# Attention's values: one TensorE product for both parts of the probabilities, with the parts' rows turned on ScalarE and added on GpSimd

## The chip, the cores and the metric

The kernel runs on one core of a Trainium2 chip. The metric is the time of one execution in device microseconds (us), the median of three. The core's engines work side by side: TensorE (PE) multiplies, VectorE (DVE), ScalarE (ACT) and GpSimd (POOL) do the elementwise work, SyncE (SP) issues the transfers.

## The reference

One decoder layer for one sequence of 256 positions, width 1024, all in float32. Cut to what matters here:

```
proj  = x @ w_in                       -> q | k | v | B | C | h | gate_attn | gate_conv
y_att = attention(q, k, v) @ W_att     8 heads of 64, causal, one block of 256 keys
y_cnv = (B * causal_dwconv3(C * h)) @ W_cnv
mix   = (sigmoid(g_att) * y_att + sigmoid(g_cnv) * y_cnv) @ W_o
x     = LayerNorm(alpha * x + mix)
u     = causal_dwconv3(x @ W_up);  f = (silu(u_gate) * u_val) @ W_down
x     = LayerNorm(alpha * x + f)
```

With 256 positions there is no earlier block, so attention is softmax(q k^T / 8) v over the keys up to the query's own position. The step that is changed is the last product of it: probabilities times values, and how its result gets from PSUM to the operand `aT` of the product with W_att.

## The kernel before

**Two parts of every operand.** To keep float32 accuracy with TensorE's shorter format, each operand is split into a high part (a copy, which rounds) and a low part (what the rounding left). For weights ScalarE makes the high part `wh` (line 221 of the profile) and VectorE the low part `wl` (line 231), from the loaded `raw`. `mm3` then makes three products: high by high, high by low, low by high (lines 336, 337, 338). The operands on the other side (`xT`, `yT`, `aT`, `mT`, `x1T`) are split in the same way: high on ScalarE, low on VectorE (lines 250 and 254).

**Units and slots.** The weights are a list of units of 128 rows by 1024 words. `slot(u)` writes one unit's TensorE products and then, in a fixed order, what the other engines do beside them: ScalarE's work of the slot's first half ("act"), the next `wh`, ScalarE's second half ("act2"), VectorE's first half ("first"), the next `wl`, VectorE's second half ("dve"). Each engine runs its own list strictly in this order; a wait holds all that stands behind it. The table `STEPS` says in which half-slot (twice the unit's number, plus one for a second half) each stage of attention, of the convolution and of the gates stands. Units 0 to 11 of this table are the products for h, C and B, units 12 to 27 those for the gates `g`, from 28 on those for `y` (y_att and y_cnv), then come W_o (`o`), and the feed-forward part (`u`, `d`, `e`).

**Attention's values.** The eight heads go in four pairs p of two heads j. `vp[:, t, p, js]` holds, for 128 keys (t), 128 columns: 64 of V's high part and 64 of its low part. `PT[:, a, j, :]` holds the transposed probabilities of head j, high part (a = 0) and low part (a = 1): 256 queries for the first 128 keys, 128 queries for the second. `attend(p)` makes eight products per pair into one PSUM bank: for each head, both parts of the probabilities with 256 words, and both with 128, all summed onto each other. The result has 128 rows: the upper 64 from V's high part, the lower 64 from V's low part. `attend_out` (ScalarE) copies the lower 64 rows of both heads to the upper rows of a scratch tile `ac`; `attend_sum` (VectorE) adds them to the upper rows that are still in PSUM, one head to each half of the tile's rows; `attend_h` (ScalarE) and `attend_l` (VectorE) make `aT`'s two parts from it. The attention products stand in the slots of units 13, 19, 22 and 24.

**What is near in the program.** `m` (line 874) sums the gated branches on VectorE; ScalarE puts `m` into 16-bit halves (`mix`, line 880), a transposing transfer turns them, ScalarE joins them (`mw`, line 888) and makes `mT`; TensorE's W_o products read `mT`. Behind those come the first LayerNorm and `x1T`, which the feed-forward products read. GpSimd does little: memsets, three masks (`affine_select`), one power per LayerNorm (`pow`, line 968), and four adds of `fs` near the end (line 1315).

Of the kernel before, what the change touches and what calls it, by code (L numbers as in the profile page):

```python
# [13 lines left out]
AF = mybir.ActivationFunctionType  # L14
ALU = mybir.AluOpType

P = 128
S = 256
# [3 lines left out]
HD = 64  # L22
# [128 lines left out]
def layer_kernel(ctx: ExitStack, tc: tile.TileContext, x, wpack, cpack, b_gate, ln1_g, ln1_b, ln2_g, ln2_b, out):  # L151
    nc = tc.nc
# [13 lines left out]
    def ps_bank(name):  # L166
        return ps_pool.tile([P, 512], F32, tag="ps", name=name)

    def scratch(shape, name, bufs=None, tag="scr"):
        return tmp.tile(shape, F32, tag=tag, name=name, bufs=bufs or 5)  # L170
# [190 lines left out]
    vp = vpt[:, 0:2048].rearrange("p (t g n) -> p t g n", t=2, g=4)  # L361
    PT = vpt[:, 2048:3584].rearrange("p (a j n) -> p a j n", a=2, j=2)
# [51 lines left out]
    SB, SM, PR = {}, {}, {}  # L414
# [77 lines left out]
    def attend(p):  # L492


        o = PR[p, "o"] = ps_bank(f"av{p}").rearrange("p (j s) -> p j s", j=2)
        for j in range(2):
            js = slice(j * P, (j + 1) * P)
            for a in range(2):
                nc.tensor.matmul(o[:, j], vp[:, 0, p, js], PT[:, a, j, 0:256], start=a == 0, stop=False)
            for a in range(2):  # L500
                nc.tensor.matmul(o[:, j, P:S], vp[:, 1, p, js], PT[:, a, j, 256:384], start=False, stop=a == 1)

    def attend_out(p):

        c = PR[p, "c"] = scratch([P, 2, S], f"ac{p}")
        nc.scalar.activation(c[0:HD], PR[p, "o"][HD:P], AF.Copy)

    def attend_sum(p):
        c, o = PR[p, "c"], PR[p, "o"]
        nc.vector.tensor_tensor(c[HD:P, 0], o[0:HD, 1], c[0:HD, 1], op=ALU.add)  # L510
        nc.vector.tensor_tensor(c[0:HD, 0], o[0:HD, 0], c[0:HD, 0], op=ALU.add)

    def attend_h(p):
        nonlocal aT
# [11 lines left out]
    def at(u, part, f, *a):  # L526
        beside.setdefault(u, {}).setdefault(part, []).append((f, a))
# [44 lines left out]
    def open_ps():  # L572
# [5 lines left out]
    STEPS = dict(vl=[3, 0],  # L578
             qw=[5, 7, 9, 13],
             qwE=[1, 1, 1, 0],  # L580
             qh=[7, 9, 11, 14],
             ql=[6, 9, 12, 16],
             s=[5, 11],
             m=[13, 17, 23, 24],
             e=[15, 21, 24, 31],
             n=[17, 23, 33, 37],
# [4 lines left out]
             av=[13, 19, 22, 24],  # L591
             out=[26, 39, 44, 49],
             sum=[35, 42, 49, 51],
             ah=[41, 47, 50, 54],
             al=[44, 52, 53, 55],
             c1=[21, 35],
             c2a=[23, 26, 38, 41],
             c2d=[25, 29, 41, 44],
# [16 lines left out]
    def on(engine, step, f, *a):  # L615
        u, part = divmod(step, 2)
        at(C0 + u, (("act", "act2"), ("first", "dve"))[engine][part], f, *a)
# [13 lines left out]
    for p in range(4):  # L631
        on(1, STEPS["m"][p], masked, p)
        on(0, STEPS["e"][p], exps, p)
        on(1, STEPS["n"][p], normalize, p)
        on(1, STEPS["n"][p], probs_halves, p)
        on(1, STEPS["n"][p], probs_T, p)
        on(STEPS["wE"][p], STEPS["w"][p], probs_words, p)
        on(0, STEPS["h"][p], probs_h, p)
        on(1, STEPS["l"][p], probs_l, p)
        at(C0 + STEPS["av"][p], "pe", attend, p)  # L640
        on(0, STEPS["out"][p], attend_out, p)
        on(1, STEPS["sum"][p], attend_sum, p)
        on(0, STEPS["ah"][p], attend_h, p)
        on(1, STEPS["al"][p], attend_l, p)

# [600 lines left out]
    for k, (kind, i, u) in enumerate(seq[:tail_from]):  # L1246
        if k == half_steps:
            hold.clear()
        if kind == "h":
            c, v, t = i  # L1250
# [11 lines left out]
        elif kind == "u":  # L1262
            c, v = i
# [142 lines left out]
```

## Time and profile before

| what | value |
|---|---|
| median of three runs | 354.62 us (354.11 to 354.84) |
| profiled execution | 354.48 us |
| its span, first to last instruction | 352.7 us |
| PE busy | 345.2 us (98%), 1603 products |
| DVE busy | 298.9 us (85%) |
| ACT busy | 245.7 us (70%) |
| POOL busy | 8.4 us (2%) |
| mean granted TensorE clock | 0.997 |

The profile comes from one execution, 354.48 us long; 1.8 us of it lie outside the span. "Busy" is the time in which an engine had an instruction in work. A row of a timeline gives the start, the time from the first start to the last end of the instructions put together in it, the engine, the line, the operation, the tile it writes and those it reads, the shape, the count, and in brackets how long the engine was idle before it and who released it. Matmuls are pipelined, so a product's row is longer (0.39 us) than the distance to the next one.

### The profile page before, as it was taken

How to read it: one execution, taken by the hardware profiler on the slowest of the kernel's cores; microseconds unless marked ns; L12 is line 12 of the kernel's file. 1: busy time of each engine (PE TensorE's matmuls, PEld its weight loads, DVE VectorE, ACT ScalarE, POOL GpSimd, SP SyncE). 2: the span in 40 equal slices, each digit the busy share in tenths (PEclk: the TensorE clock that was granted, in tenths of full speed). 3: DMA queues.
4: the chain of work that ended last, by engine and by line, in shares of the span. 5: the costliest groups of instructions: out<-in, count | busy, mean ns of one | idle time of the engine just before them, and what ended most of it. 6: DMA issues, size and time to landing. Idle time of an engine off the chain costs nothing.

```text
span 352.7 us, 4599 instructions
## 1 busy us (share of the span) xinstructions
PE 345.2 (98%) x1603; PEld 287.0 (81%) x1603; DVE 298.9 (85%) x508; ACT 245.7 (70%) x370; POOL 8.4 (2%) x29
## 2 busy tenths in 40 slices
PE   9999999999999999999999999999999999999992
PEld 8788888888888888888888888888888888888882
DVE  4797787999989998879867879999999879796985
ACT  3776948789896767856496658688686867758700
POOL 1000000000001000000100000000000000000120
PEclk9999999999999999999999999999999999999998
DMA  7999886779867899993298199779969987753002
GB/s 250 422 418 362 181 282 243 147 271 226 199 185 242 336 367 256 315 259 119 47 305 186 24 335 309 284 162 315 321 128 413 260 256 242 200 210 61 0 30 90
DMA packets 56070, 81.63 MB, mean 231 GB/s; under 512 B 45552, under 2 KB 46192, under 8 KB 49008
## 3 DMA queue, kind: packets, MB, share of 16 engines
q1 hardware_dynamic: 56048, 81.35, 74.1%
q8 instruction: 12, 0.20, 0.2%
q14 instruction: 10, 0.08, 0.1%
HBM read 69.28 MB, written 1.05 MB: 199 GB/s over the span
## 4 chain that ended last, share of the span: by engine, by line
PE 90%; issue 3%; DVE 3%; ACT 2%; POOL 1%; POOLq 0%; DVEq 0%
PE u L336 11%; PE u L337 11%; PE u L338 11%; PE qk L677 6%; PE g L336 4%; PE g L337 4%; PE g L338 4%; PE v L677 3%; PE d L337 3%; PE d L336 3%; PE d L338 3%; PE o L338 2%; PE o L337 2%; PE y L338 2%; PE y L337 2%
## 5 line engine op out<-in xcount | busy, mean ns | idle before, releaser
L231 DVE TENSOR_TENSOR wl<-raw,wh 128x1024 fp32r<-128x1024 f32 x104 | 125.0, 1217 | 15.6 <-ACT wh L221 15.4
L221 ACT ACTIVATE wh<-raw 128x1024 fp32r<-128x1024 f32 x102 | 103.9, 1051 | 3.4 <-DMA raw<-in_wpack 3.4
L336 PE MATMUL u<-wh,x1T 128*128 128x512 f32 x176 | 68.5, 389 | 0.0
L337 PE MATMUL u<-wl,x1T 128*128 128x512 f32 x176 | 68.5, 389 | 0.0
L338 PE MATMUL u<-wh,x1T 128*128 128x512 f32 x176 | 68.5, 389 | 0.0
L338 PEld LDWEIGHTS u<-wh,x1T 128*128 128x128 f32 x176 | 33.0, 188 | 6.9
L336 PEld LDWEIGHTS u<-wh,x1T 128*128 128x128 f32 x176 | 33.0, 188 | 6.9
L337 PEld LDWEIGHTS u<-wl,x1T 128*128 128x128 f32 x176 | 33.0, 188 | 6.8
L1050 ACT ACTIVATE fc<-pb,consts 128x256 f32<-128x256 f32 x44 | 20.0, 503 | 24.0 <-DVE pb L1092 24.0
L336 PE MATMUL d<-wh,f 128*128 128x512 f32 x76 | 29.6, 389 | 0.0
L337 PE MATMUL d<-wl,f 128*128 128x512 f32 x76 | 29.6, 389 | 0.0
L338 PE MATMUL d<-wh,f 128*128 128x512 f32 x76 | 29.6, 389 | 0.0
L1083 ACT ACTIVATE up<-u 128x1024 uint16<-128x1024 uint16 x22 | 21.4, 1012 | 6.2 <-PE u L338 6.2
L336 PE MATMUL g<-wh,xT 128*128 128x512 f32 x64 | 25.3, 395 | 0.0
L337 PE MATMUL g<-wl,xT 128*128 128x512 f32 x64 | 25.0, 390 | 0.0
L338 PE MATMUL g<-wh,xT 128*128 128x512 f32 x64 | 24.9, 389 | 0.0
L1058 DVE SCALAR_TENSOR_TENSOR fc<-pb,consts,fc 128x254 f32<-128x254 f32 x44 | 21.3, 483 | 1.6
L1056 DVE SCALAR_TENSOR_TENSOR fc<-pb,consts,fc 128x255 f32<-128x255 f32 x44 | 21.0, 477 | 0.9 <-ACT fc L1050 0.9
L254 DVE TENSOR_TENSOR wl<-raw,wh 128x512 fp32r<-128x512 f32 (+2 forms) x23 | 20.4, 929 | 1.6 <-ACT wh L253 1.4
L253 ACT ACTIVATE wh<-raw 128x512 fp32r<-128x512 f32 (+2 forms) x23 | 17.6, 815 | 2.5 <-DMA raw<-in_wpack 2.5
L677 PE MATMUL qk<-wh,xT 128*128 128x512 f32 x60 | 19.2, 390 | 0.0
L1092 DVE COPY pb<-up 128x1024 uint16<-128x1024 uint16 x22 | 16.5, 749 | 1.9 <-DMA up<-up 1.8
(207 smaller groups left out, 608.7 us busy)
## 6 DMA issues: line engine op xcount, KB each, us to landing
raw<-in_wpack SPq DMA_DIRECT2D x55, 1024.0 KB, 5.6
raw<-in_wpack SPq DMA_DIRECT2D x6, 896.0 KB, 11.4
bg<-in_b_gate SPq DMA_DIRECT2D x4, 256.0 KB, 5.1
xr<-in_x SPq DMA_DIRECT2D x1, 1024.0 KB, 8.3
ln<-in_ln_g SPq DMA_DIRECT2D x2, 512.0 KB, 6.3
ln<-in_ln_b SPq DMA_DIRECT2D x2, 512.0 KB, 7.1
raw<-in_wpack SPq DMA_DIRECT2D x3, 256.0 KB, 4.0
raw<-in_wpack SPq DMA_DIRECT2D x1, 512.0 KB, 6.3
```

The source lines that it names most:

```text
L221: nc.scalar.activation(units[u]["h"], raw_of(u), AF.Copy)
L231: nc.vector.tensor_tensor(units[u]["l"], raw_of(u), units[u]["h"].bitcast(F32), op=ALU.subtract)
L253: nc.scalar.activation(h, src, AF.Copy)
L254: (eng or nc.vector).tensor_tensor(l, src, h.bitcast(F32), op=ALU.subtract)
L336: nc.tensor.matmul(o, ah, bh, start=start, stop=False)
L337: nc.tensor.matmul(o, ah, bl, start=False, stop=False)
L338: nc.tensor.matmul(o, al, bh, start=False, stop=stop)
L677: nc.tensor.matmul(banks[m][t], (xl if p == 2 else xh)[:, k, t * P:(t + 1) * P], wl if p == 1 else wh, start=k == 0 and p == 0, stop=k == ...
L1050: nc.scalar.activation(PB["c", i][:, a], PB[i][:, a * S:(a + 1) * S], AF.Copy, scale=w_ffn(2, j))
L1056: nc.vector.scalar_tensor_tensor(c[:, 1:S], pb[:, a * S:a * S + S - 1], w_ffn(1, j), c[:, 1:S], op0=ALU.mult, op1=ALU.add)
L1058: nc.vector.scalar_tensor_tensor(c[:, 2:S], pb[:, a * S:a * S + S - 2], w_ffn(0, j), c[:, 2:S], op0=ALU.mult, op1=ALU.add)
L1083: nc.scalar.activation(half.rearrange("p (w n) -> p w n", w=2), PB["rows", c][t].bitcast(U16).rearrange("p (n w) -> p w n", w=2), AF.Copy)
```

## The change

`attend` now gives each head a bank of its own and streams both parts of the probabilities through the columns of V in one product: 512 words for the first 128 keys, and two runs of 128 words for the second. The bank then holds, side by side, the sums with the probabilities' high part and with their low part, 128 rows each. `attend_out` copies the low-part halves of both heads to `ac` (two ScalarE copies of 128 rows by 256), `attend_sum` adds the high-part halves to them (two VectorE adds of 128 rows by 256). A new function `attend_turn` brings the lower 64 rows of `ac` up (one ScalarE copy, 64 rows by 512) and adds them to the upper ones in two GpSimd adds of 64 rows by 256; head 1's result goes to the lower half of the rows as before. `STEPS` places `attend_turn`, and places `attend_h` and `attend_l` anew. Other lines move down by 8 (L231 stays, L841 becomes L849, and so on).

```
     def attend(p):
-        o = PR[p, "o"] = ps_bank(f"av{p}").rearrange("p (j s) -> p j s", j=2)
+        o = PR[p, "o"] = [ps_bank(f"av{p}_{j}").rearrange("p (a s) -> p a s", a=2) for j in range(2)]
         for j in range(2):
             js = slice(j * P, (j + 1) * P)
-            for a in range(2):
-                nc.tensor.matmul(o[:, j], vp[:, 0, p, js], PT[:, a, j, 0:256], start=a == 0, stop=False)
-            for a in range(2):
-                nc.tensor.matmul(o[:, j, P:S], vp[:, 1, p, js], PT[:, a, j, 256:384], start=False, stop=a == 1)
+            nc.tensor.matmul(o[j], vp[:, 0, p, js], PT[:, :, j, 0:256], start=True, stop=False)
+            nc.tensor.matmul(o[j][:, :, P:S], vp[:, 1, p, js], PT[:, :, j, 256:384], start=False, stop=True)
     def attend_out(p):
         c = PR[p, "c"] = scratch([P, 2, S], f"ac{p}")
-        nc.scalar.activation(c[0:HD], PR[p, "o"][HD:P], AF.Copy)
+        for j in range(2):
+            nc.scalar.activation(c[:, j], PR[p, "o"][j][:, 1], AF.Copy)
     def attend_sum(p):
         c, o = PR[p, "c"], PR[p, "o"]
-        nc.vector.tensor_tensor(c[HD:P, 0], o[0:HD, 1], c[0:HD, 1], op=ALU.add)
-        nc.vector.tensor_tensor(c[0:HD, 0], o[0:HD, 0], c[0:HD, 0], op=ALU.add)
+        for j in range(2):
+            nc.vector.tensor_tensor(c[:, j], o[j][:, 0], c[:, j], op=ALU.add)
+    def attend_turn(p):
+        c = PR[p, "c"]
+        low_rows = scratch([P, 2, S], f"al{p}")
+        nc.scalar.activation(low_rows[0:HD], c[HD:P], AF.Copy)
+        for j in (1, 0):
+            nc.gpsimd.tensor_tensor(c[j * HD:j * HD + HD, 0], c[0:HD, j], low_rows[0:HD, j], op=ALU.add)
...
-             ah=[41, 47, 50, 54],
-             al=[44, 52, 53, 55],
+             turn=[36, 44, 50, 52],
+             ah=[41, 48, 53, 56],
+             al=[44, 52, 56, 57],
...
+        on(0, STEPS["turn"][p], attend_turn, p)
```

On TensorE, the values of the first pair stand between two products of the gates; these were the rows before (`av` is the bank, `vpt` holds V's columns and the probabilities):

```order
L499 MATMUL av_875<-vpt 128x256 x2
L501 MATMUL av_875<-vpt 128x128 x2
L499 MATMUL av_875<-vpt 128x256 x2
L501 MATMUL av_875<-vpt 128x128 x2
```

And these stand in the same place now:

```order
L498 MATMUL av_0_875<-vpt 128x512
L499 MATMUL av_0_875<-vpt 128x2x128
L498 MATMUL av_1_876<-vpt 128x512
L499 MATMUL av_1_876<-vpt 128x2x128
```

Eight products became four, with as many words in all; nothing else on TensorE moved.

On VectorE, this is the stretch from the sums of the third pair on, before (`ac_1050`, `ac_1124` and `ac_1187` are the scratch tiles of the second, third and fourth pair; 128x1024 rows are weights' low parts):

```order
L510 TENSOR_TENSOR ac_1187<-av_1170,ac_1187 64x256
L511 TENSOR_TENSOR ac_1187<-av_1170,ac_1187 64x256
L250 TENSOR_TENSOR aT<-ac_1050,aT 128x256
L231 TENSOR_TENSOR wl_1233<-raw_1046,wh_1185 128x1024
L250 TENSOR_TENSOR aT<-ac_1124,aT 128x256
L250 TENSOR_TENSOR yT<-ct_1044,yT 128x2x256
L231 TENSOR_TENSOR wl_1254<-raw_1046,wh_1230 128x1024
L250 TENSOR_TENSOR aT<-ac_1187,aT 128x256
L841 TENSOR_TENSOR gates<-g_1156,bg_1101 128x512
L841 TENSOR_TENSOR gates<-g_1157,bg_1101 128x512
L231 TENSOR_TENSOR wl_1270<-raw_1093,wh_1251 128x1024
```

And now (`ac_1049`, `ac_1125`, `ac_1186` are the same three pairs):

```order
L510 TENSOR_TENSOR ac_1186<-av_0_1171,ac_1186 128x256
L510 TENSOR_TENSOR ac_1186<-av_1_1172,ac_1186 128x256
L250 TENSOR_TENSOR aT<-ac_1049,aT 128x256
L231 TENSOR_TENSOR wl_1241<-raw_1045,wh_1184 128x1024
L250 TENSOR_TENSOR yT<-ct_1043,yT 128x2x256
L231 TENSOR_TENSOR wl_1260<-raw_1045,wh_1237 128x1024
L250 TENSOR_TENSOR aT<-ac_1125,aT 128x256
L849 TENSOR_TENSOR gates<-g_1157,bg_1101 128x512
L849 TENSOR_TENSOR gates<-g_1158,bg_1101 128x512
L231 TENSOR_TENSOR wl_1277<-raw_1093,wh_1257 128x1024
L250 TENSOR_TENSOR aT<-ac_1186,aT 128x256
```

VectorE has as many instructions as before. The low part of `aT` for the third pair moved behind `yT` and a weight; that for the fourth pair behind two gate adds and a weight.

On ScalarE, this is the stretch of the third and fourth pair now (`al` is the tile of the turned rows; L523 writes `aT`'s high part, L852 the gates):

```order
L505 ACTIVATE ac_1186<-av_0_1171 128x256
L505 ACTIVATE ac_1186<-av_1_1172 128x256
L515 ACTIVATE al_1210<-ac_1125 64x512
L814 ACTIVATE yT<-ct_1043 128x2x256
L852 ACTIVATE gates<-gates 128x512 x2
L515 ACTIVATE al_1233<-ac_1186 64x512
L221 ACTIVATE wh_1237<-raw_1045 128x1024
L523 ACTIVATE aT<-ac_1125 128x256
L221 ACTIVATE wh_1257<-raw_1093 128x1024
L523 ACTIVATE aT<-ac_1186 128x256
```

The turning copies (L515) are new, the copies out of PSUM (L505) are two per pair in place of one, and each high part of `aT` stands one weight or more behind the turn that feeds it.

## Rows read from the trace of the kernel before

**Rows 1.** The page: busy time of the engines, share of the span, instructions.

```profile
PE 345.2 (98%) x1603; PEld 287.0 (81%) x1603; DVE 298.9 (85%) x508; ACT 245.7 (70%) x370; POOL 8.4 (2%) x29
```

**Rows 2.** Windows: stretch, length, busy time of PE, PEld, DVE, ACT, POOL.

```profile
106.10:122.70 16.60, 16.60 (x83) 14.02 (x82) 16.51 (x24) 11.86 (x18) 1.16 (x2) 1.00 0.78 281
```

**Rows 3.** Timeline of TensorE around the first pair's values.

```profile
79.37 0.39 PE L338 MATMUL g<-wh,xT 128*128 128x512 f32 x1
...
80.29 0.34 PE L501 MATMUL av<-vpt 128*128 128x128 f32 x2
80.46 0.45 PE L336 MATMUL g<-wh,xT 128*128 128x512 f32 x1
80.75 0.40 PE L337 MATMUL g<-wl,xT 128*128 128x512 f32 x1
80.98 0.39 PE L338 MATMUL g<-wh,xT 128*128 128x512 f32 x1
```

**Rows 4.** Timeline of TensorE at products of 256 words, near the end.

```profile
344.13 0.28 PE L1178 MATMUL e<-wl,f 128*128 128x256 f32 x1
...
344.49 0.28 PE L1178 MATMUL e<-wl,f 128*128 128x256 f32 x1
```

**Rows 5.** Timeline of VectorE, from before the second pair's sums to behind the fourth pair.

```profile
97.91 0.69 DVE L250 TENSOR_TENSOR yT<-ct,yT 128x512 fp32r<-128x512 f32 x1 [1.26 <-ACT yT L806]
...
103.09 0.99 DVE L795 SCALAR_TENSOR_TENSOR ct<-z,consts,ct 128x256 f32<-128x256 f32 x2
104.10 0.42 DVE L510 TENSOR_TENSOR ac<-av,ac 64x256 f32<-64x256 f32 x1
104.53 0.42 DVE L511 TENSOR_TENSOR ac<-av,ac 64x256 f32<-64x256 f32 x1
...
111.67 2.44 DVE L231 TENSOR_TENSOR wl<-raw,wh 128x1024 fp32r<-128x1024 f32 x2
...
121.07 0.41 DVE L250 TENSOR_TENSOR aT<-ac,aT 128x256 fp32r<-128x256 f32 x1
121.40 1.27 DVE L841 TENSOR_TENSOR gates<-g,bg 128x512 f32<-128x512 f32 x2
122.60 1.20 DVE L231 TENSOR_TENSOR wl<-raw,wh 128x1024 fp32r<-128x1024 f32 x1
```

**Rows 6.** Timeline of ScalarE: the second pair's copy out of PSUM.

```profile
107.10 0.59 ACT L506 ACTIVATE ac<-av 64x512 f32<-64x512 f32 x1 [1.33 <-PE av L501]
```

**Rows 7.** GpSimd by line and shape: count | busy us, mean ns | idle before.

```profile
L1315 POOL TENSOR_TENSOR fs<-fs 128x256 f32<-128x256 f32 x3 | 2.2, 738 | 163.9 <-ACT fs L1312 163.8
L1315 POOL TENSOR_TENSOR fs<-fs 128x128 f32<-128x128 f32 x1 | 0.5, 462 | 0.1
```

**Rows 8.** Timeline of GpSimd: a mask alone, one beside VectorE's work, and the adds.

```profile
1.29 0.29 POOL L270 TENSOR_SCALAR_AFFINE_SELECT mask<-mask 128x128 f32<-128x128 f32 x1
...
112.08 0.95 POOL L953 TENSOR_SCALAR_AFFINE_SELECT ident<-ident 128x128 f32<-128x128 f32 x1
...
334.12 2.79 POOL L1315 TENSOR_TENSOR fs<-fs 128x256 f32<-128x256 f32 x4 [163.80 <-ACT fs L1312]
```

**Rows 9.** The line of the weights' low parts: ns minimum, median, maximum.

```profile
L231 DVE TENSOR_TENSOR wl<-raw,wh x104: 1178/1217/1309, 41.5 to 332.3; 128x1024 fp32r<-128x1024 f32 x104
```

**Rows 10.** Timeline of VectorE: one operation, without GpSimd's adds and beside them.

```profile
165.66 0.68 DVE L983 SCALAR_TENSOR_TENSOR xr<-xr,o 128x512 f32<-128x512 f32 x1
...
335.10 0.68 DVE L983 SCALAR_TENSOR_TENSOR x<-x,d 128x512 f32<-128x512 f32 x1
```

**Rows 11.** Timeline of ScalarE: the first mix, waiting for the gated sums.

```profile
129.23 1.06 ACT L880 ACTIVATE mix<-m 128x1024 uint16<-128x1024 uint16 x1 [3.12 <-DVE m L874]
```

**Rows 12.** Timeline of VectorE: the first operand of the feed-forward part.

```profile
164.46 1.28 DVE L254 TENSOR_TENSOR x1T<-x1t,x1T 128x512 fp32r<-128x512 f32 x2
```

**Rows 13.** Timeline of TensorE: two products that read what VectorE makes.

```profile
126.67 0.39 PE L338 MATMUL y<-wh,aT 128*128 128x512 f32 x1
...
166.36 0.39 PE L338 MATMUL u<-wh,x1T 128*128 128x512 f32 x1
```

## The prediction

> **What bounds the kernel now.** I read the page first. TensorE is busy 345.2 of 352.7 us, VectorE 298.9, ScalarE 245.7, GpSimd 8.4 [rows 1]. So any product that gets shorter comes out of the time one for one, as long as the operands still arrive in time. The windows come second, for the stretch that the change touches: TensorE is busy all of its 16.60 us, VectorE 16.51, ScalarE 11.86, GpSimd 1.16 [rows 2]. The reader should see that TensorE waits for nothing, that VectorE is full and works ahead of TensorE by a stock of finished operands: it doesn't hold TensorE yet, but each us that it loses stays lost until that stock is eaten.
>
> **TensorE's part.** From the product ahead of the values at 79.37 to the first regular one at 80.75 it is 1.38 us now [rows 3]. A product of 512 words takes 0.23 (80.75 to 80.98); three of 256 words take 0.36, so 0.12 each [rows 4]. Afterwards the same stretch holds four steps of 0.227 (the product ahead, two of 512 words, the product behind) and two of 256 words: 4 x 0.227 + 2 x 0.12 = 1.15. That saves 0.23 for a pair, **0.93 us** for four. What goes is not words (there are as many) but the slow steps behind short products: 0.29 (80.46 to 80.75) where 0.23 is usual [rows 3]. The trace of before has no product of this kind with two runs on both sides. If it cost like two of 128 words (0.17, from 80.29 to 80.46), the gain would be 0.93 - 8 x 0.05 = 0.53 us; it can hardly be above 0.95. I take 0.93, because words alone set the step of the 256-word products [rows 4].
>
> **ScalarE's part.** New per pair: two copies of 128x256 in place of one of 64x512 (0.59, [rows 6]), and the turn, which has that copy's shape. I estimate 0.2 more for the copies and 0.5 for the turn, 0.7 us a pair. ScalarE has it: ahead of the second pair's copy it waits 1.33 us [rows 6], and the window leaves 16.60 - 11.86 = 4.7 us free [rows 2], against 2.1 us for three pairs. Cost: nothing. Without that cover it would be up to 2.1 us on ScalarE, and what is queued behind the turn is `wh`, for which VectorE's `wl` and TensorE wait.
>
> **VectorE's part.** Same count. The sums have twice the rows but the same 256 words, so 0.42 each. Now they start 0.43 apart (104.10, 104.53) and the first starts 0.02 behind its neighbour's end at 103.09 + 0.99, while other neighbours overlap by 0.08 (121.07 + 0.41 against 121.40) [rows 5]. They write different halves of the rows today, and the same rows in two regions afterwards. If that is what keeps them apart, each pair gains about 0.17 (0.10 at the first, 0.09 at the second), **0.5 us** over pairs two to four. The bounds are 0 and 0.55.
>
> `aT` low for the fourth pair goes behind two gate adds and a weight. It ends at 121.48 now; the gates and the weight behind it run to 122.60 + 1.20 = 123.80 [rows 5], so it would end about there, or 123.3 with the gain. TensorE reads it at 126.67 [rows 13], less 0.93: 125.74. That leaves 2.4 us.
>
> **GpSimd's part.** Eight adds of 64x256. An add of 256 words takes 0.738 us and one of 128 takes 0.462 [rows 7]: 2.16 ns a word, so 0.55 us is data and 0.19 start. GpSimd is nearly idle, so its own time is no matter. What matters is what the adds do to VectorE. Two places bear on that. A mask of 128x128 took 0.29 us alone, and 0.95 us at 112.08 beside two weights' low parts; those two took 2.44 us together, which fits the longest of all 104 (1309 ns) and a median one (1217) less that overlap [rows 5, 8, 9]. So GpSimd waits for VectorE, then VectorE for GpSimd, here 0.09 us. And beside the four `fs` adds, an operation of VectorE that reads one operand from PSUM took 0.68 (335.10), as it does without them [rows 8, 10]. I read this as: only VectorE operations with both operands in SBUF (`wl`, and the low parts of `aT`, `yT`, `vpt`) lose time.
>
> The mask reads 128 words, an add 2 x 256. By words the price is 4 x 0.092 = 0.37 us an add. If VectorE loses the whole of an add's data time less the usual overlap of 0.08, it is 0.47; the bounds are 0 and 0.74, the whole add. I take 0.4, near the row that shows a loss at all.
>
> How many of the eight hit such work? The first pair's two fall where VectorE waits for ScalarE (1.26 us ahead of 97.91, [rows 5]). The second pair's (about 106.2) meet a weight and a low part. Of the third pair's, one falls largely beside the fourth pair's sums, which read PSUM. The fourth pair's meet `yT` and a weight. I count 4.5, so 4.5 x 0.4 = **1.8 us** on VectorE.
>
> The Trainium skill, "SBUF — State Buffer", section "Who interferes with whom", speaks against this change: VectorE and GpSimd share one pair of ports as an exclusive lock, a VectorE instruction with two SBUF inputs contends with a GpSimd one that reads SBUF, and whoever issues first holds it for the whole instruction while the other blocks fully. The trace agrees that one side waits (the mask's 0.95 for 0.29), but the 0.09 lost by VectorE is less than the mask's whole 0.29. By the rule in full the price would be an add's 0.74 and the kernel would be slower; that is a rival below.
>
> **How much VectorE may lose.** A delay there travels: ScalarE's first `mix` waits 3.12 us for the gated sum `m` [rows 11]; behind it come the transfer, `mw`, `mT`, the W_o products and `x1T`. The first low part of `x1T` ends at 164.46 + 0.68 = 165.14 and TensorE reads it at 166.36 [rows 12, 13]: 1.22 us of lead, the smallest on this path that I found. So VectorE may lose 1.22 + 0.5 = 1.72 us before the time is later than before; if it loses less, the time falls by the rest, up to TensorE's 0.93.
>
> **Sum.** Change = the larger of -0.93 and (VectorE's loss - 1.72) = 1.8 - 1.72 = +0.08. 354.48 + 0.08 = 354.56. The profiled execution is 0.14 below the median of the runs shown, so I say **354.6 us: no change that shows**. A kernel of this length can tell about 0.2%, 0.71 us, from no change.
>
> **Rivals.**
>
> 1. *The adds cost VectorE little, the full gain stays.* For it: one row alone shows a loss, and a small one. If an add costs 0.17 or less, the loss is under 0.79 and all of 0.93 comes out: 353.6. Up to 0.25 an add, it is still faster by over 0.71. Against it: the mask, with a quarter of the words, already cost 0.09.
>
> 2. *The adds hold VectorE for their whole time: slower.* At 0.55 an add it is 4.5 x 0.55 - 1.72 = +0.76, 355.2; at 0.74 it is 3.33 - 1.72 = +1.6, 356.1. It decides from 0.57 an add on, or from 0.43 if six adds are hit. Near 2.4 us of loss `aT` of the fourth pair comes too late as well, at the `y` products about 126. For it: GpSimd's own row shows full waiting. Against it: 0.09 measured.
>
> 3. *The output product with two runs costs like two of 128 words.* TensorE then gains 0.53 only. With VectorE's loss at 1.8 the time is the same, 354.6, since the late operand sets it; with a small loss it is 354.0, within the bound.
>
> 4. *VectorE's sums gain nothing.* Then the sum is 1.8 - 1.22 = +0.58, 355.1, still within the bound, and rival 2 begins at 0.43 an add.
>
> **How the numbers follow.** Middle case with rivals 3 and 4: 0.42. Rival 1: 0.33. Rival 2, with what rival 4 adds to it: 0.25. Those are also same, faster, slower. The range takes in rival 1's full gain (353.55) with the spread of the runs, and rival 2 as far as 355.8; below and above I leave some 0.2. The likeliest case's own range is 353.9 to 355.3.
>
> **What the profile would show.** The values' stretch should fall from 1.38 to about 1.15, with the products behind at 0.23. VectorE's two sums should overlap. A weight's low part near 106 to 108 and 119 to 123 should show longer than 1.22, by 0.3 to 0.5, in four or five places, and GpSimd's adds well over 0.74. TensorE should wait a few tenths between the `y` products and the first `u` products. If it waits nowhere, rival 1 holds; if over 1.5 us, rival 2. What would make the prediction wrong outright: a ScalarE queue held up by `attend_h`, which now waits for GpSimd, with `wh` behind it.

## The result and the profile after

| kernel | median | against before, 95% interval |
|---|---|---|
| before | 354.41 us (354.11 to 354.84) | |
| changed | 356.57 us (355.98 to 356.96) | 1.0058 (1.0046 to 1.0070) |

Slower by about 2 us: beyond the range, which goes up to 355.8, and not "no change". The profiled execution took 356.72 us with a span of 354.9, against 354.48 and 352.7.

Where the time went is read best from TensorE, which still does its list in one order. The table sets the start of the first product of each part in the two timelines side by side; a step in the last column is time lost or won in the part ahead of it.

| first product of | before, us | after, us | difference |
|---|---|---|---|
| `h` | 37.89 | 38.07 | +0.18 |
| `y` (behind all values) | 121.46 | 120.86 | -0.60 |
| the transposes of x1, behind most W_o products | 162.27 | 162.72 | +0.45 |
| `u` | 165.91 | 166.53 | +0.62 |
| the first `d` | 209.43 | 210.53 | +1.10 |
| the last stretch of `d` | 318.23 | 319.33 | +1.10 |
| the row mean, behind the last `d` products of 512 words | 342.03 | 344.50 | +2.47 |

So 0.78 us was won at the values, 1.22 lost between `y` and `u`, 0.48 in the first `u` products, and 1.37 near the end, 200 us behind the change. The prediction has a gain and a loss at the first three of these places, and nothing at the last.

The page's lines for the engines, to set beside [rows 1]:

```profile
PE 346.4 (98%) x1587; PEld 285.1 (80%) x1587; DVE 301.6 (85%) x508; ACT 248.5 (70%) x378; POOL 16.7 (5%) x37
```

VectorE has the same 508 instructions and 2.7 us more of busy time (301.6 against 298.9).

The timeline of TensorE at the first pair's values, answering [rows 3]:

```profile
79.54 0.39 PE L338 MATMUL g<-wh,xT 128*128 128x512 f32 x1
79.77 0.39 PE L498 MATMUL av<-vpt 128*128 128x512 f32 x1
79.99 0.28 PE L499 MATMUL av<-vpt 128*128 128x256 f32 x1
80.11 0.40 PE L498 MATMUL av<-vpt 128*128 128x512 f32 x1
80.34 0.28 PE L499 MATMUL av<-vpt 128*128 128x256 f32 x1
80.46 0.40 PE L336 MATMUL g<-wh,xT 128*128 128x512 f32 x1
80.70 0.40 PE L337 MATMUL g<-wl,xT 128*128 128x512 f32 x1
```

From 79.54 to 80.70 it is 1.16 us where it was 1.38. A product with two runs on both sides takes 0.12, as one of 256 words in one run does. This step of the prediction holds.

The timeline of VectorE, answering [rows 5] (the normalization that the first pair's adds meet, the second pair's sums, and what the adds of the second to the fourth pair meet):

```profile
94.15 1.96 DVE L461 TENSOR_SCALAR sm<-sm,st 128x128 f32<-128x128 f32 x4
...
103.92 0.75 DVE L510 TENSOR_TENSOR ac<-av,ac 128x256 f32<-128x256 f32 x2
...
105.83 2.90 DVE L231 TENSOR_TENSOR wl<-raw,wh 128x1024 fp32r<-128x1024 f32 x2
108.65 1.50 DVE L250 TENSOR_TENSOR vpt<-sm,vpt 128x768 fp32r<-128x768 f32 x1
...
118.06 1.76 DVE L231 TENSOR_TENSOR wl<-raw,wh 128x1024 fp32r<-128x1024 f32 x1
119.74 1.23 DVE L250 TENSOR_TENSOR yT<-ct,yT 128x512 fp32r<-128x512 f32 x1
120.90 1.76 DVE L231 TENSOR_TENSOR wl<-raw,wh 128x1024 fp32r<-128x1024 f32 x1
```

Three of these instructions before the change:

```profile
94.36 1.01 DVE L461 TENSOR_SCALAR sm<-sm,st 128x128 f32<-128x128 f32 x4
...
106.12 2.35 DVE L231 TENSOR_TENSOR wl<-raw,wh 128x1024 fp32r<-128x1024 f32 x2
108.46 0.96 DVE L250 TENSOR_TENSOR vpt<-sm,vpt 128x768 fp32r<-128x768 f32 x1
```

And GpSimd's timeline beside it, after the change:

```profile
94.08 1.61 POOL L517 TENSOR_TENSOR ac<-ac,al 64x256 f32<-64x256 f32 x2 [91.92 <-ACT al L515]
106.52 2.81 POOL L517 TENSOR_TENSOR ac<-ac,al 64x256 f32<-64x256 f32 x2 [10.83 <-ACT al L515]
116.76 1.98 POOL L517 TENSOR_TENSOR ac<-ac,al 64x256 f32<-64x256 f32 x2 [7.43 <-ACT al L515]
119.48 2.10 POOL L517 TENSOR_TENSOR ac<-ac,al 64x256 f32<-64x256 f32 x2 [0.74 <-ACT al L515]
```

A weight's low part that takes 1.22 elsewhere takes 1.76 here, `yT` 1.23 for 0.69, `vpt` 1.50 for 0.96, a pair of weights 2.90 for 2.35: five times 0.54 or 0.55. Each lies beside a GpSimd add; two adds, 1.48 us by [rows 7], take up to 2.81. The two sums (0.75 together) now overlap. The first pair's adds, which the prediction let fall into a wait, meet the normalization: its four instructions take 1.96 in place of 1.01. But VectorE's wait behind it, 1.26 us at 97.91 [rows 5], is gone: this `yT` now starts at 97.12, and the second pair's sums at 103.92 in place of 104.10. So this stretch cost nothing in the end.

How it reaches TensorE, in ScalarE's timeline, answering [rows 11]:

```profile
131.18 1.06 ACT L888 ACTIVATE mix<-m 128x1024 uint16<-128x1024 uint16 x1 [3.45 <-DVE m L882]
```

That is 131.18 - 129.23 = 1.95 us later. And in TensorE's waits after the change (for what, us in all, times, longest; `d` belongs to the loss near the end):

```profile
PEld o L338 <- DVE mT L250: 1.1, 2, 0.7
...
PEld d L336 <- ACT f L1078: 0.6, 1, 0.6
PEld u L338 <- DVE x1T L254: 0.6, 1, 0.6
```

The low parts of `mT` and `x1T` come too late, which is the chain that the prediction followed.

The loss near the end is elsewhere. VectorE's timeline there, where the last turned `up` is put together (line 1100):

```profile
323.93 1.22 DVE L231 TENSOR_TENSOR wl<-raw,wh 128x1024 fp32r<-128x1024 f32 x1
326.85 0.75 DVE L1100 COPY pb<-up 128x1024 uint16<-128x1024 uint16 x1 [1.71 <-DMA up<-up]
```

VectorE waits 1.71 us for the transposing transfer. Before, there was no wait:

```profile
324.12 0.76 DVE L1092 COPY pb<-up 128x1024 uint16<-128x1024 uint16 x1
```

ScalarE's `f` is late next, and TensorE waits for it at the last `d` products. The DMA view of that transfer's time, after (a row per queue: packets, MB, share of the stretch; then issues with the time to landing; stretch 321.7 to 325.7):

```profile
q1 hardware_dynamic: 2112, 0.52, 68.7%
q8 instruction: 1, 0.02, 1.7%
issues: line engine op xcount, KB each, median us to landing
up<-up SPq DMA_TRANSPOSE x2, 4.1
```

Before (stretch 320.6 to 323.6) the same 2112 packets are alone and land in 3.2 us:

```profile
q1 hardware_dynamic: 2112, 0.52, 90.2%
issues: line engine op xcount, KB each, median us to landing
up<-up SPq DMA_TRANSPOSE x2, 3.2
```

The new thing is one packet of 16 KB on queue 8, "instruction". Before, such a packet was over ahead of the transfer: the stretch 318 to 320.5 of that trace has the packet and none of the transfer's. How it delays the transfer can be seen from 324.5 to 325.7 after the change. In the 1.3 us ahead of 324.5 the transfer moves 1007 of its 2112 packets; in these 1.2 us it moves its last 26:

```profile
q8 instruction: 1, 0.02, 5.6%
q1 hardware_dynamic: 26, 0.00, 2.2%
```

### The profile page after: what moved, and what is told of

The parts are those of the page before. It is cut to its first block, busy times and chain, and to the rows that moved or that the text cites. A ratio compares the mean times of both kernels' runs of the same rounds, so it can differ in the third digit from the quotient of the medians.

```text
span 354.9 us, 4586 instructions
## 1 busy us (share of the span) xinstructions
PE 346.4 (98%) x1587; PEld 285.1 (80%) x1587; DVE 301.6 (85%) x508; ACT 248.5 (70%) x378; POOL 16.7 (5%) x37
## 3 DMA queue, kind: packets, MB, share of 16 engines
HBM read 69.28 MB, written 1.05 MB: 198 GB/s over the span
## 4 chain that ended last, share of the span: by engine, by line
PE 43%; DVE 4%; issue 3%; DMA 1%; POOL 1%; ACT 1%; DVEq 0%; POOLq 0%
PE u L338 11%; PE u L336 11%; PE u L337 11%; PE d L336 3%; PE d L338 3%; PE d L337 3%; DMA up<-up 1%; DVE wl L231 1%; POOL fs L1323 1%; DVE wl L254 1%; DVE fc L1064 0%; DVE fc L1066 0%; ACT fs L1320 0%; ACT up L1091 0%; DVE res L1371 0%
## 5 line engine op out<-in xcount | busy, mean ns | idle before, releaser
L231 DVE TENSOR_TENSOR wl<-raw,wh 128x1024 fp32r<-128x1024 f32 x104 | 126.7, 1234 | 15.2 <-ACT wh L221 15.0
```

The lines of the kernel that those rows point to most:

```text
L231: nc.vector.tensor_tensor(units[u]["l"], raw_of(u), units[u]["h"].bitcast(F32), op=ALU.subtract)
```

## The experiments

Three theories were to be told apart. **P**: GpSimd's adds stop VectorE. **O**: the order costs, ScalarE waiting at the turn and `aT`'s parts standing later. **F**, for the loss near the end, was set up when experiments 1 to 4 were in: the packet on queue 8 is a load of TensorE's program; with 16 products fewer it comes later and falls into the last transfer.

**1. The changed kernel again** (no edit).

> The changed kernel once more, for the last microseconds of its profile. There the last transposing transfer of `up` landed about 1.4 us later than before and TensorE lost 1.36 us in the last `d` products. Theory C (chance): in this profile the `d` products from 318 us on lose nothing, and the time is about 355.3. Theory S (it follows from the change, because the transfer starts 1.1 us later): the loss is there again, about 1.3 us, and the time 356.5.

357.78 us, ratio 1.0105 (1.0076 to 1.0134). The loss in the last `d` products is there again (1.35 us), so it isn't chance. The reason that the expectation gave, that the transfer starts later, falls with experiment 2: there it starts at 318.81, ahead of the 319.47 of the kernel before, and the loss is there (1.26 us). This time there is one more, at the `y` products:

```profile
125.57 0.39 PE L337 MATMUL y<-wl,aT 128*128 128x512 f32 x1
126.72 0.50 PE L338 MATMUL y<-wh,aT 128*128 128x512 f32 x1 [0.76 <-DVE aT L250]
```

GpSimd's timeline says why:

```profile
116.48 3.72 POOL L517 TENSOR_TENSOR ac<-ac,al 64x256 f32<-64x256 f32 x2 [7.43 <-ACT al L515]
```

The third pair's adds took 3.72 us in place of 1.98: the second of them took 2.67 in place of 0.93, while VectorE did a low part of `aT`, a weight's and `yT`'s, none of them stretched. ScalarE's turn of the fourth pair waited 2.13 us for it, the weights' high parts behind it were late, and VectorE, full until then, waited 2.38 us for one. So the price depends on which engine holds up the other. That parts the two profiled executions (356.72 and 357.68 us); that it also parts the two sets of runs, 356.57 and 357.78, is likely and not shown.

**2. Without the adds.**

```
-        for j in (1, 0):
-            nc.gpsimd.tensor_tensor(c[j * HD:j * HD + HD, 0], c[0:HD, j], low_rows[0:HD, j], op=ALU.add)
```

> The changed kernel without its eight GpSimd adds (the lower rows, values by V's low part, are then left out of the sums); everything else stays, ScalarE's turn too. Theory P (GpSimd's adds stop VectorE for 0.55 us each): every weight's low part takes 1.22 again, TensorE waits nowhere between 120 and 170 us, the 0.77 us that TensorE gained at the values stay: 353.7 (353.3 to 354.1). Theory O (the order: ScalarE waits 2.8 us at the turn of the third pair, and aT's parts stand later): the waits between 120 and 170 remain, 355.5 or more.

354.88 us, ratio 1.0010 (0.9998 to 1.0021): not shown to differ from the kernel before. The weights' low parts are all whole again (maximum 1229 ns), and TensorE waits nowhere between `y` and `d`:

```profile
L231 DVE TENSOR_TENSOR wl<-raw,wh x104: 1180/1218/1229, 41.6 to 333.2; 128x1024 fp32r<-128x1024 f32 x104
```

The turn and the order are still those of the change, so O falls, and P holds for the stretch from 120 to 210 us. But the time isn't the 353.7 that P alone gives: the loss near the end remains without any add.

**3. The adds on VectorE** (`gpsimd` made `vector` in the line above).

> The eight adds on VectorE in place of GpSimd, at the same places. Theory P: VectorE pays about 0.34 us an add (0.42 less the overlap) in place of 0.55, and nothing else is stretched: VectorE is late at the first mix by about 1.5 us in place of 1.95, time about 355.0 (354.4 to 355.7), less than with GpSimd. Theory O: as the changed kernel, 356.5, since the order is the same. If moving work off VectorE helped at all, it would be slower than the changed kernel.

360.78 us, ratio 1.0179 (1.0138 to 1.0220), more than 4 us over what either theory gave. VectorE's adds take 0.85 us a pair, little as reckoned, but they stand in VectorE's list ahead of the turn's end:

```profile
DVE ac L517 <- ACT al L515: 6.3, 4, 2.9
```

VectorE waits 6.3 us for ScalarE, and TensorE 2.07 us for a weight at 111.46. The run doesn't compare the prices of an add on the two engines; it shows that in this order the adds on VectorE bring the wait for the turn with them, which GpSimd's own list had kept away from VectorE.

**4. GpSimd writes and doesn't read.**

```
-            nc.gpsimd.tensor_tensor(c[j * HD:j * HD + HD, 0], c[0:HD, j], low_rows[0:HD, j], op=ALU.add)
+            nc.gpsimd.memset(low_rows[j * HD:j * HD + HD], 0.0)
```

> In place of each GpSimd add one GpSimd memset of 64 rows by 512 words (about 0.5 us, writes SBUF, reads nothing; it fills the turned rows, so the lower rows are left out of the sums). Theory P with reading as the cause: no VectorE instruction is stretched, the time is that without adds, 353.7. Theory P with any GpSimd access as the cause: the low parts are stretched by up to 0.5 us again, 355 to 356.5.

355.23 us, ratio 1.0018 (1.0008 to 1.0028), with the loss near the end (1.23 us) and no other. No low part is stretched (maximum 1227 ns) and the normalization takes 1.01 again, though each memset lasts 0.52 us beside them. Writing alone costs VectorE nothing here; with experiment 5, it is GpSimd's reading that counts.

**5. GpSimd reads one operand.**

```
-            nc.gpsimd.tensor_tensor(c[j * HD:j * HD + HD, 0], c[0:HD, j], low_rows[0:HD, j], op=ALU.add)
+            nc.gpsimd.tensor_copy(low_rows[HD:P, j], low_rows[0:HD, j])
```

> The changed kernel with each GpSimd add replaced by a GpSimd copy of 64 rows by 256 words out of the turned tile (one input in place of two; the lower rows are left out of the sums). If VectorE is stopped for as long as GpSimd reads, a stretched weight's low part takes 1.22 + 0.28 in place of 1.22 + 0.55, VectorE loses about 1.4 us, inside its lead: time as without adds, 354.9. If it is stopped for the copy's whole time whatever that reads, the stretch is the copy's full duration, 0.3 to 0.4 us. If any read costs 0.55: 356.5.

355.54 us, ratio 1.0021 (1.0010 to 1.0032). The lines of VectorE that meet the copies:

```profile
105.50 2.55 DVE L231 TENSOR_TENSOR wl<-raw,wh 128x1024 fp32r<-128x1024 f32 x2
107.98 1.15 DVE L250 TENSOR_TENSOR vpt<-sm,vpt 128x768 fp32r<-128x768 f32 x1
...
119.13 1.41 DVE L231 TENSOR_TENSOR wl<-raw,wh 128x1024 fp32r<-128x1024 f32 x1 [0.27 <-ACT wh L221]
```

Each is 0.20 us longer, where an add cost 0.54; the expectation had 0.28 for the time of reading and 0.3 to 0.4 for the whole copy. A copy takes 0.40 us where VectorE doesn't hold it (at 119.07), the mask 0.29 alone [rows 8], an add 0.74 [rows 7]. Take off the add's start, 0.19, and 0.21, 0.10 and 0.55 are left; VectorE lost 0.20, 0.09 [rows 5, 9] and 0.54. So what VectorE lost is GpSimd's time on the data, without its start; that the copy and the mask have the add's start is an assumption. Not every copy cost that much: the normalization took 1.26 in place of 1.01 beside two of them, and beside the one at 118.08 it was GpSimd that waited (1.05 us for the copy, 0.68 for `yT`).

TensorE loses 0.48 at `x1T` here and 1.3 near the end. The 0.48 isn't the copies': the first `mix` starts at 129.06, no later than before (129.23), and the last `mw` then waits 4.98 us for its transposing transfer, where it waited 4.19 before.

**6. The kernel before with the adds as extra work** (the new turn and two GpSimd adds per pair at the places of the change, into a tile that nobody reads):

```
+        nc.scalar.activation(low_rows[0:HD], c[0:HD], AF.Copy)
+        for j in (1, 0):
+            nc.gpsimd.tensor_tensor(low_rows[HD:P, j], c[0:HD, j], low_rows[0:HD, j], op=ALU.add)
```

> The kernel before, with the new turn and eight GpSimd adds as extra work at the places of the changed kernel, into a tile that nobody reads. Theory P (an add stops a VectorE instruction that reads SBUF twice for 0.55 us): five or six such instructions are stretched by 0.5 to 0.6, VectorE is about 2.8 us late at the first mix, TensorE waits at the W_o products and x1T for 1.2 to 1.8 us; no loss at the end, as TensorE's list is the old one: 356.0 (355.3 to 356.9). If it's the new order of aT's parts that costs: 354.6 to 354.9.

356.71 us, ratio 1.0056 (1.0040 to 1.0073). The old products, the old order of `aT`, and 0.55 us more at five places (two further low parts of `aT` take 0.95 as well):

```profile
105.86 2.90 DVE L231 TENSOR_TENSOR wl<-raw,wh 128x1024 fp32r<-128x1024 f32 x2
108.68 1.49 DVE L250 TENSOR_TENSOR vpt<-sm,vpt 128x768 fp32r<-128x768 f32 x1
...
118.19 0.96 DVE L250 TENSOR_TENSOR aT<-ac,aT 128x256 fp32r<-128x256 f32 x1
```

TensorE waits for the low parts of `mT` and `x1T` as in the changed kernel and loses 1.68 us from `y` to the first `d`, where the changed kernel lost 1.70. It loses 0.53 more at 225, where a weight's low part is late; VectorE had waited 2.56 us for a transfer of `up` at 194.9 (1.55 before), and why that was late stays open. Near the end it waits for nothing. Nobody reads these adds, so it isn't a wait for their results that costs; and the loss near the end isn't theirs.

**7. The kernel before with a shorter list for TensorE.** The warm-up's words in half as many products:

```
-            nc.tensor.matmul(warm[:, 0:P], some, some, start=True, stop=True)
-    warm_up(31)
+            nc.tensor.matmul(warm[:, 0:2 * P], some, wide, start=True, stop=True)
+        nc.tensor.matmul(warm[:, 0:P], some, some, start=True, stop=True)
+    warm_up(15)
```

> The kernel before, with its warm-up of 31 TensorE products of 128 words made as 15 of 256 and one of 128: as many words, 15 products and 15 weight loads fewer in TensorE's list, nothing else changed. Theory F (the changed kernel has 16 products fewer, so each 16 KB load of TensorE's program comes about 3.6 us later, and the last one, at 319.1 us before the change, falls into the last transposing transfers of `up`): the load comes at about 322.5, the transfers end about 1 us later, TensorE loses 1.2 to 1.4 us in the last `d` products, time 355.8. Without F: 354.6, no loss at the end.

356.03 us, ratio 1.0035 (1.0023 to 1.0047). Nothing changed but TensorE's first 3 us, and the kernel loses 1.2 us at 334. The DMA view from 321.1 to 325.1 has the packet inside the transfer:

```profile
q8 instruction: 1, 0.02, 1.4%
...
up<-up SPq DMA_TRANSPOSE x2, 4.0
```

F holds. TensorE lost 0.46 us more at `x1T`, where `mw` waited 5.26 us for its transposing transfer and a load at 153.0 took 2.38 us; that these two belong together was not tried.

**8. Without adds, with TensorE's list made as long as before** (warm-up of 47 products, 15 of 128 words and 32 of 64).

> The changed kernel without its eight GpSimd adds (lower rows left out of the sums), and with a warm-up of 47 products (15 of 128 words, 32 of 64) in place of 31, as many words, so that TensorE's list is as long as before the change. Theory F: the last load is ahead of the transfers again, the 1.2 us at the end are gone, and the 0.77 us from the values stay: 353.7 (353.3 to 354.1). Without F: 354.9, as without adds.

353.82 us, ratio 0.9967 (0.9956 to 0.9978). With both causes gone, TensorE waits for nothing from 75 us on, and what is left is the gain at the values (0.78 us ahead at `y`, 0.82 at the row mean, counted from `h`).

**9. The whole changed kernel with the longer list.**

> The whole changed kernel with the longer warm-up list. Theory F: its time less 1.3 us, 355.2 to 356.4, with no loss in the last `d` products; the waits between 120 and 170 us stay. Without F: 356.5 to 357.8.

355.65 us, ratio 1.0037 (1.0015 to 1.0059). No loss near the end: the transfer lands in 3.3 us. The waits for `mT` and `x1T` stay, and 0.72 us are lost between 221 and 225, as in experiment 6 behind a late transfer of `up` (VectorE waits 3.22 us for it at 194.9). Its runs lie between 354.48 and 357.83; the varying waits of experiment 1 would spread them, but only one of them was profiled.

All fourteen profiles, those of the kernel before and of the experiments below included, agree. In the seven with the shorter list (the changed kernel and experiments 1 to 5 and 7) the load meets the end of the last transfer, which lands in 4.0 to 4.1 us; in the seven with a list as long as before the load is over before the transfer's first packet, and it lands in 3.1 to 3.3.

**10. The products of a pair in another order, kernel before** (256 and 128 words by turns).

> The kernel before with the eight products of a pair in another order: 256 and 128 words by turns in place of two and two. If the slow steps (0.17 for a product of 256 words, 0.28 for one of 512) stand behind two short products in a row and one short product alone leaves time for the next weight load, a pair takes 0.05 to 0.1 us less, and the kernel 0.2 to 0.4: 354.3. If every short product has its slow step, no change or up to 0.2 more.

354.46 us, ratio 0.9996 (0.9986 to 1.0007): no change. The steps moved and didn't go: from the product ahead to the first regular one it is 80.64 - 79.26 = 1.38 us as before, each short product followed by its slow step.

**11. Two pairs in the new form, their adds beside the gate adds.** First and second pair by the new functions, third and fourth by the old; the warm-up of 39 products keeps TensorE's list as long as before.

```
-             turn=[36, 44, 50, 52],
-             ah=[41, 48, 53, 56],
-             al=[44, 52, 56, 57],
+             turn=[38, 47],
+             ah=[41, 50, 51, 54],
+             al=[44, 52, 53, 55],
```

> A version that should beat both: the new products for the first and second pair alone, their turns moved so that GpSimd's adds fall beside VectorE's gate adds, which read PSUM (turn in half-slots 38 and 47, the second pair's high part of aT in 50); third and fourth pair as before; the warm-up made 8 products longer with as many words, so that TensorE's list keeps its length. If both causes are right (adds stop only VectorE instructions that use SBUF alone; the program load must not move), TensorE gains half of 0.77, VectorE loses less than its lead, and nothing is lost at the end: 354.6 - 0.4 = 354.2 (353.8 to 354.6). If the adds miss the gate adds, VectorE is stretched as before and the time is 354.6 or more.

354.26 us, ratio 0.9994 (0.9981 to 1.0006). In its profile the first pair's adds stretch no weight and the second pair's meet one pair of weights (3.00 us in place of 2.35), TensorE wins 0.38 us at the values, and waits for nothing behind them.

> The version with two pairs once more, to narrow its interval: its first profile has TensorE 0.38 us ahead from the second pair on, VectorE stretched at one place, and nothing lost at the end. If that is the whole difference, the ratio lies at 0.9989 (354.2) again; if the first runs were luck, at 1.000.

354.25 us, ratio 0.9991 (0.9978 to 1.0004). Both sets lie near where 0.38 us would put them, and neither interval excludes no change. No version here is shown to beat the kernel before.

## Why the prediction was wrong

Two steps failed. The price of an add was sized at 0.4 us and is 0.54, so that VectorE lost 2.7 us where 1.8 was expected; that alone makes the kernel slower, and still inside the range. And that TensorE's list gets shorter by 16 products was counted as a gain alone, with nothing set against it; it cost 1.37 us near the end, and this took the time out of the range.

**TensorE's gain: right in kind.** Predicted 0.93 us. Each stretch fell by 0.22, 0.88 in all, and at `y` 0.78 us is left (0.60 and the 0.18 of the start). The other 0.1 lies behind the pairs: from the second product behind the first pair to the fifteenth it was 2.96 us (80.75 to 83.71) and is 2.99 (80.70 to 83.69). Rival 3 is out.

**VectorE's sums and ScalarE's extras: right.** The sums overlap (0.75 for two). ScalarE waited 2.83 us at the third pair's turn and 3.45 at the first mix, and nothing came from it in the profiled execution; in experiment 1 the turn, waiting for GpSimd, did hold up the weights, much as the prediction had named it (with `attend_h` in the place of the turn) as what would make it wrong outright.

**The price of an add: the step that failed first.** The prediction took 0.4 us, by scaling the mask's 0.09 with the words read (4 x 0.092). The runs show 0.54. The scale that fits is GpSimd's own time on the data, 0.10 us for the mask and 0.55 for an add, which could be had from [rows 7, 8]. The prediction had this reading as the second of two, at 0.47, and the whole data time at 0.55 as rival 2's price.

The Trainium skill, "SBUF — State Buffer", section "Who interferes with whom", has an exclusive lock for the whole instruction. The runs agree in that only GpSimd's reads matter to an instruction with two SBUF inputs (experiments 4 and 5). They differ in the length: VectorE lost 0.54 of an add's 0.74. That whoever issues first wins, as the same section of the Trainium skill has it, doesn't come out of the rows' starts: the third pair's second add started 0.25 us ahead of the weight's low part in the first profile (117.81 and 118.06) and 0.26 ahead in experiment 1 (117.53 and 117.79); in the first the weight was stretched, in the second the add waited.

**The count: nearly right, and partly by luck.** Predicted 4.5, found five at 0.54 behind 105 us. The first pair's adds were to cost nothing because they fall into VectorE's wait. They fell on the normalization ahead of it and stretched that by 0.95; the wait then took this up, so the nothing was right and its reason wrong. The prediction had taken from one row that a VectorE instruction with one SBUF operand doesn't lose time. That row read its other operand from PSUM; the normalization reads and writes SBUF alone. The same page of the Trainium skill says of `tensor_scalar` that it can use both of VectorE's port pairs and then contends; this trace agrees for the adds, 1.96 us for 1.01, while beside memsets it stayed at 1.01 (experiment 4).

**How much VectorE may lose: right.** With the measured price, five stretches of 0.55 and 0.1 for the mask are 2.85 us, and 2.85 - 1.72 = +1.13. Measured from `h` to the first `d` it is 1.10 - 0.18 = +0.92. So that sum gives 355.4 to 355.6: rival 2 as it was written, and inside the range. The lead of 1.22 can be read too: the low part of `x1T` starts 2.09 us later than before (166.55 against 164.46), the product that reads it 0.93 (167.29 against 166.36), and 2.09 - 1.22 is 0.87. And TensorE's loss from `y` to the first `d`, 1.70 us, is over the 1.5 that the prediction had set as rival 2's sign. (By rival 2's own reckoning, rival 4 would move its limit to 0.46 an add, not to 0.43; nothing hangs on it.)

**What the prediction didn't have: the end.** The other 1.37 us come from TensorE's program. Sixteen products fewer, with their weight loads, move every 16 KB load of the rest; the last goes from 319.1 us to 324.5, into the end of the last transposing transfer, which lands 0.9 us later, and the tail of the kernel hangs on it. Experiments 7 and 8 show this cause from both sides: it costs 1.2 us with nothing else changed, and without it and the adds the gain of the values is there. No row of the prediction shows these loads.

## What to carry to other kernels

GpSimd is not a free engine beside a full VectorE: in this kernel an instruction of it that read SBUF either stopped a VectorE instruction that used SBUF alone, by 0.54 us for an add of 256 words and 0.20 for a copy, or was held up itself, with ScalarE waiting behind it. Scale such a price by GpSimd's own time on the data, and give it work that VectorE's PSUM instructions stand beside, or that only writes. And where a change alters the number of an engine's instructions, see in the DMA view where its program loads fall, since one in a transfer that the end waits for can cost more than the change wins.

## What the runs showed of the hardware that was not expected

- One 16 KB load of TensorE's program at the end of the last transposing transfers made them land in 4.0 to 4.1 us in place of 3.1 to 3.3, and TensorE lost 1.2 to 1.5 us behind them.
- GpSimd memsets of 0.52 us stretched no VectorE instruction; where VectorE gave way, copies of 256 words cost it 0.20 us and adds 0.54, each about GpSimd's time without its start.
- In two executions of the same kernel two of GpSimd's adds took 1.98 and 3.72 us beside the same work of VectorE; the medians of the two sets of runs were 356.57 and 357.78 us.
